# The experts' stage as a row of weight-unit steps in a fixed order, with float32 weights left unsplit in two down blocks of the light experts

## The chip, the cores and the metric

One NeuronCore of a Trainium2 chip runs the kernel. The engines are TensorE (PE in the profile, with PEld for its weight loads), VectorE (DVE), ScalarE (ACT), GpSimd (POOL) and the DMA queue that SyncE (SP) feeds. The metric is the time of one execution on the device in microseconds (us), as the median of repeated runs.

## The reference

Two encoder layers over 256 tokens of width 1024. Each has a token mixer, a cross-attention and a feed-forward part; in the second layer the feed-forward part is eight experts, of which each token uses two:

```python
def swiglu(t, w_gu, w_down):
    a, g = jnp.split(t @ w_gu, 2, axis=-1)
    return (jax.nn.silu(a) * g) @ w_down

def moe_swiglu(h, w_router, w_gu, w_down):
    ...
    top_logit, top_idx = lax.top_k(logits, TOP_K)
    ...
    for e in range(N_EXPERTS):
        out = out + gate[:, e:e + 1] * swiglu(t, w_gu[e], w_down[e])
```

Everything is float32. An expert's weights are 1024 x 5632 (gate and up) and 2816 x 1024 (down): 34.6 MB that have to be read whatever the number of tokens.

## The kernel before

**Split weights.** A product in float32 accuracy is built from `float32r` products (the profile writes fp32r). Each weight piece arrives by DMA in a buffer `raw`; ACT copies it rounded into `hi` (L216), DVE subtracts to get `lo = raw - hi` (L220), and TensorE multiplies with both. Pools give six buffers each for `hi` and `lo`, of 128 x 1024 elements, which is three units' worth; in the arm that ran there are nine buffers `raw` during the first expert and seven afterwards.

**Units.** A unit is one 1 MB piece (four blocks of 128 rows by 512 columns), so two pieces of `hi` and two of `lo`. An expert has six hidden blocks j; block 5 is half as wide. Per block there are two units of gate weights (tile `pm`, called g below), two of up weights (a) and two of down weights (d, tile `py`): 36 units an expert, six of them half as large, and 66 splits each on ACT and DVE.

**Heavy and light.** The experts are sorted by their number of tokens. The first three (heavy, up to 128 tokens) hold their activations as two parts and use three products per weight block (`mm3`, L234 to L236). The last five (light, up to 64 tokens) place high part and low part side by side in the 128 columns of one operand, so that two products do (`stream`, L915 and L916). The lower half of the result is then added to the upper one: ACT copies it out (`low`, L969) and a product with an identity adds it (L970). After that come `silu` on ACT (L950), the product `h` on DVE (L951), a transposition on PE (L954), and its split into `hTh` and `hTl` on ACT and DVE (L256 and L257).

**Pairs.** Two experts at a time, the tokens are collected by products with a selection matrix (`gather`, tiles `pg`, `xg`) and given back by another one (`scatter`, tile `psct`).

**Order.** The code writes an expert's work block by block. What stands behind a product (`low`, `silu`, ...) is put on the list `later` and run by `flush` after the splits of the next units have been written. The scheduler of the language decides the final order within each engine. DMA issues stand on SP's queue and wait only for a free buffer `raw`.

Of the kernel before, what the change touches and what calls it, by code (L numbers as in the profile page):

```python
# [21 lines left out]
DFF, E = 2816, 8  # L22
# [7 lines left out]
PLAIN = ()  # L30
# [126 lines left out]

class K:
# [29 lines left out]
    def unit(self, src, base, pk, c, g, blocks=False, whole=False):  # L188

# [8 lines left out]
        if isinstance(base, int):  # L198
            w = bass.AP(tensor=src.tensor, offset=src.offset + base + pk.off[c, g], ap=[[n, 128], [1, n]])
        else:  # L200

            o = base[1] + pk.off[c, g]
            w = src.rearrange("(e n) -> e n", e=E)[bass.ds(base[0], 1), o:o + 128 * n]
            w = w.rearrange("o (p n) -> (o p) n", p=128)
        nc.sync.dma_start(raw.rearrange("p k c -> p (k c)"), w)
        if whole:
            return [(k0, kn, raw)]
# [630 lines left out]
    def experts(self, c, pos, gs, xs, acc, A, ahead, full, early=()):  # L838


        down, self.later = None, []
        for e in range(E):
            if e % 2 == 0:
                pair = ahead
            name = self.nc.values_load(self.of[0:1, e:e + 1], engines=[mybir.EngineType.SP], min_val=0, max_val=E - 1)
            one = dict(pair, e=e, i=e % 2, xe=pair["xg"][e % 2], light=e >= full, name=name)
            for j in range(6):
                if e == 1 and j == 0:
# [6 lines left out]
                if e % 2 and e < E - 1 and j == 1:  # L855
                    ahead = self.gather(c, e + 1, pos, xs, A, full)
        self.down(*down, gs, acc, A)
        while self.later:
            self.flush()

    def gather(self, c, e, pos, xs, A, full):


        nc = self.nc
        half = CAP // 2
        light = [e + i >= full for i in range(2)]
        sl = A.tile([128, 2, 2, CAP], FR, name="sl")
        for t in range(2):
            for i in range(2):
                at = pos[:, t, e + i:e + i + 1]  # L870
                if light[i]:
                    nc.vector.tensor_scalar(sl[:, t, i].rearrange("p (a b) -> p a b", a=2),  # L872
                                            self.io[:, None, :half].to_broadcast([128, 2, half]), at, None,
                                            op0=OP.is_equal)
                else:
                    nc.vector.tensor_scalar(sl[:, t, i], self.io[:, CAP * c:CAP * c + CAP], at, None, op0=OP.is_equal)

        xg = []
        for i in range(1 if all(light) else 2):
            pool, tag = self.xgs[0]  # L880
            xg.append(pool.tile([128, 2, 8, CAP], FR, name="xg", tag=tag, bufs=1))
            self.xgs.append(self.xgs.pop(0))
        xg = [xg[0][:, i] for i in range(2)] if all(light) else [z[:, 0] if l else z for z, l in zip(xg, light)]
        p = [None, None]
        for k in range(8):
            for i in range(2):
                if k % 2 == 0:
                    p[i] = self.mm.tile([128, 2, 2 * CAP], FT, name="pg", tag="mm")
                for t in range(2):
                    nc.tensor.matmul(p[i][:, k % 2], xs[i][:, t, k * 128:k * 128 + 128],  # L890
                                     sl[:, t].rearrange("p a b -> p (a b)"), start=not t, stop=bool(t))
            if k % 2:
                ks = slice(k - 1, k + 1)
                for i in range(2):
                    for z, copy in ((0, lambda o, v: nc.scalar.activation(o, v, AF.Copy)),
                                    (1, nc.vector.tensor_copy)):
                        if light[i]:
                            cs = slice(z * half, (z + 1) * half)
                            copy(xg[i][:, ks, cs], p[z][:, :, i * CAP:i * CAP + CAP][:, :, cs])
                        else:  # L900
                            copy(xg[i][:, z, ks], p[z][:, :, i * CAP:i * CAP + CAP])
        st = A.tile([128, 2, S], FR, name="st")
        p = self.ps.tile([128, 2, S], FT, name="pst", tag="t")
        for i in range(2):
            for t in range(2):
                nc.tensor.transpose(p[:, i, t * 128:t * 128 + 128], f32(sl[:, t, i]), self.idn)
        nc.vector.tensor_copy(st, p)
        return dict(sl=sl, st=st, xg=[[z] if l else [z[:, 0], z[:, 1]] for z, l in zip(xg, light)])

    def stream(self, ps, x, k, w, first, last):  # L910

        if len(x) == 2:
            self.mm3(ps, [z[:, k] for z in x], w, first, last)
        else:
            self.nc.tensor.matmul(ps, x[0][:, k], w[0], start=first, stop=False)  # L915
            self.nc.tensor.matmul(ps, x[0][:, k], w[1], start=False, stop=last)  # L916

    def up(self, x, j, A):

        nc, I = self.nc, self.I  # L920
        light = x["light"]
        n = P_GU.chunks[2 * j][1]
        nb = n // 128

        def product(c):
            p = self.mm.tile([128, 512], FT, name="pm", tag="mm")
            u = self.chunk(I["we"], (x["name"], 0), P_GU, c)
            self.flush()
            for k0, kn, hi, lo in u:
                for k in range(kn):  # L930
                    self.stream(p[:, :n], x["xe"], k0 + k, (hi[:, k], lo[:, k]), k0 + k == 0, k0 + k == 7)
            return p

        pg = product(2 * j + 1)
        if light:
            self.later.append(lambda: self.fold(pg, n, A))
        pa = product(2 * j)
        half = CAP // 2
        plain = light and j in PLAIN
        if plain:  # L940
            hT = [A.tile([128, 4, half], FT, name="hTf", bufs=2)]
        else:
            hT = [A.tile([128, 4, CAP], FR, name="hT" + z) for z in ("h" if light else "hl")]

        def rest():
            if light:
                self.fold(pa, n, A)
            m = half if light else CAP
            h = A.tile([128, 512], FT, name="h", bufs=1)
            nc.scalar.activation(h[:m, :n], pa[:m, :n], AF.Silu)  # L950
            nc.vector.tensor_tensor(h[:m, :n], h[:m, :n], pg[:m, :n], op=OP.mult)  # L951
            p = self.ps.tile([128, 4, 128], FT, name="pht", tag="t")
            for b in range(nb):
                nc.tensor.transpose(p[:, b, :m], h[:m, b * 128:b * 128 + 128], self.idn[:m, :m])  # L954
            if plain:
                nc.scalar.activation(hT[0][:, :nb], p[:, :nb, :m], AF.Copy)
            elif light:
                self.split(p[:, :nb, :m], hT[0][:, :nb, :half], hT[0][:, :nb, half:])
            else:
                self.split(p[:, :nb], *(z[:, :nb] for z in hT))  # L960

        self.later.append(rest)
        return hT

    def fold(self, ps, n, A):

        half = CAP // 2
        low = A.tile([128, 512], FR, name="low", bufs=1)
        self.nc.scalar.activation(low[half:, :n], ps[half:, :n], AF.Copy)  # L969
        self.nc.tensor.matmul(ps[:half, :n], self.one64[half:], low[half:, :n], start=False, stop=True,  # L970
                              skip_group_check=True)

    def flush(self):

        later, self.later = self.later, []
        for f in later:
            f()

    def down(self, x, j, hT, gs, acc, A):

        nc, I = self.nc, self.I
        e, i = x["e"], x["i"]
        base = (x["name"], P_GU.size)
        plain = x["light"] and j in PLAIN
        if j == 0:
            self.py = [self.ps.tile([128, 512], FT, name="py", tag="s") for _ in range(2)]
        for cc in range(2):
            u = self.unit(I["we"], base, P_DN, cc, j, whole=plain)
            self.flush()
            for k0, kn, *w in u:  # L990
# [19 lines left out]
    def scatter(self, st, e, acc, A):  # L1010
# [23 lines left out]
        if i:  # L1034
            self.later.append(add)
# [91 lines left out]
```

## Time and profile before

| | us |
|---|---|
| median of 3 runs (1634.14 to 1635.0) | 1634.14 |
| the profiled execution's own time | 1637.31 |
| span of its trace | 1635.5 |
| PE busy / DVE busy / ACT busy | 1555.5 / 1304.2 / 1030.4 |

The experts' stage runs from about 847 us to the end of the span. A busy PE is not a PE at its peak: the profile draws a product of 512 columns some 0.4 us long, while in a dense row the next one starts 0.23 us later. A group of instructions on DVE is drawn the same way, so that its rate is read from long groups.

### The profile page before, as it was taken

To read this page: it belongs to the slowest core of one execution; us is meant where nothing else is said; L and a number is where in the kernel's file an instruction comes from. 1 tells how busy PE (TensorE), PEld (TensorE's weight loads), DVE (VectorE), ACT (ScalarE), POOL (GpSimd) and SP (SyncE) were. 2 spreads that over 40 slices of the span, in tenths; PEclk is the share of its full clock that TensorE was granted. 3 is DMA by queue.
4 is the path that set the end of the run, shared out by engine and by line. 5 is a ranking of instruction groups with operands and counts; after the bars stand their busy time and mean duration, and the time that the engine had idled before them with its cause. 6 is when DMAs were issued, how large, how long until landed. Compare 5 with 4: busy or idle time off the path is not lost.

```text
span 1635.5 us, 24155 instructions
## 1 busy us (share of the span) xinstructions
PE 1555.5 (95%) x8867; PEld 1276.5 (78%) x8867; DVE 1304.2 (80%) x1936; ACT 1030.4 (63%) x1422; POOL 32.9 (2%) x28
## 2 busy tenths in 40 slices
PE   6999999999999999999969999999999999999996
PEld 5999999899998889999858878888656556555554
DVE  7877686775545886777678888898899998999897
ACT  5665444544433575545436777777878788888884
POOL 1100000000000110000000000000000000000000
PEclk9999999999999999999979999999999999999999
DMA  7424564465555533456229798898999999999994
GB/s 275 142 104 144 186 247 158 155 223 190 181 180 184 190 121 126 149 199 230 79 100 426 310 405 328 334 363 321 395 335 394 381 356 371 342 405 345 406 374 147
DMA packets 65647, 421.32 MB, mean 258 GB/s; under 512 B 7664, under 2 KB 8560, under 8 KB 19568
## 3 DMA queue, kind: packets, MB, share of 16 engines
q1 hardware_dynamic: 65520, 419.69, 68.2%
q8 instruction: 72, 1.18, 0.3%
q14 instruction: 55, 0.45, 0.1%
HBM read 418.61 MB, written 1.05 MB: 257 GB/s over the span
## 4 chain that ended last, share of the span: by engine, by line
PE 78%; DVE 10%; ACT 5%; issue 5%; DMA 2%; POOL 0%; ACTq 0%; SPq 0%; DVEq 0%
PE pm L235 15%; PE pm L234 15%; PE pm L236 15%; PE pm L916 6%; DVE lo L220 6%; PE pm L915 4%; ACT hi L216 3%; PE psc L354 2%; PE py L234 2%; PE py L236 2%; PE py L235 2%; PE ptr L383 1%; PE pd L236 1%; PE pd L234 1%; PE pd L235 1%
## 5 line engine op out<-in xcount | busy, mean ns | idle before, releaser
L220 DVE TENSOR_TENSOR lo<-raw,hi 128x1024 fp32r<-128x1024 f32 (+2 forms) x1020 | 926.7, 955 | 187.2 <-ACT hi L216 183.7
L216 ACT ACTIVATE hi<-raw 128x1024 fp32r<-128x1024 f32 x770 | 770.1, 1052 | 255.9 <-PE pm L235 92.1
L236 PE MATMUL pm<-xTh,lo 128*128 128x256 f32 x928 | 264.5, 285 | 0.0
L234 PE MATMUL pm<-xTh,hi 128*128 128x256 f32 x928 | 264.4, 285 | 0.0
L235 PE MATMUL pm<-xTl,hi 128*128 128x256 f32 x928 | 264.3, 285 | 0.0
L916 PE MATMUL pm<-lo,xg 128*128 128x512 f32 (+1 forms) x480 | 197.1, 416 | 15.2 <-DVE lo L220 13.2
L915 PE MATMUL pm<-hi,xg 128*128 128x512 f32 (+1 forms) x480 | 181.8, 386 | 0.7 <-ACT hi L216 0.7
L235 PEld LDWEIGHTS pm<-xTl,hi 128*128 128x128 f32 x928 | 177.8, 192 | 1.1
L234 PEld LDWEIGHTS pm<-xTh,hi 128*128 128x128 f32 x928 | 177.7, 191 | 1.0
L236 PEld LDWEIGHTS pm<-xTh,lo 128*128 128x128 f32 x928 | 177.9, 192 | 0.7
L916 PEld LDWEIGHTS pm<-lo,xg 128*128 128x128 f32 x480 | 91.0, 190 | 88.8 <-DVE lo L220 77.6
L235 PE MATMUL pm<-lo,xg 128*128 128x512 f32 (+1 forms) x288 | 108.7, 377 | 2.3 <-DVE lo L220 2.0
L234 PE MATMUL pm<-hi,xg 128*128 128x512 f32 (+1 forms) x288 | 108.5, 377 | 1.8 <-DVE sl L872 1.8
L236 PE MATMUL pm<-hi,xg 128*128 128x512 f32 (+1 forms) x288 | 108.1, 375 | 0.0
L916 PE MATMUL py<-lo,hTh 128*128 128x512 f32 x220 | 94.7, 433 | 12.2 <-DVE lo L220 11.6
L915 PEld LDWEIGHTS pm<-hi,xg 128*128 128x128 f32 x480 | 91.2, 191 | 18.5 <-issue 5.6
L915 PE MATMUL py<-hi,hTh 128*128 128x512 f32 x220 | 91.1, 414 | 0.2 <-ACT hi L216 0.2
L950 ACT ACTIVATE h<-pm 64x512 f32<-64x512 f32 (+3 forms) x48 | 26.9, 560 | 85.2 <-PE pm L236 69.3
L916 PEld LDWEIGHTS py<-lo,hTh 128*128 128x128 f32 x220 | 40.9, 188 | 41.2 <-DVE lo L220 34.1
L969 ACT ACTIVATE low<-pm 64x512 fp32r<-64x512 f32 (+1 forms) x60 | 33.5, 558 | 61.4 <-PE pm L916 58.6
L235 PEld LDWEIGHTS pm<-lo,xg 128*128 128x128 f32 x288 | 54.9, 191 | 13.6 <-DVE lo L220 4.0
L234 PEld LDWEIGHTS pm<-hi,xg 128*128 128x128 f32 x288 | 54.8, 190 | 12.4 <-issue 2.0
(321 smaller groups left out, 2645.1 us busy)
## 6 DMA issues: line engine op xcount, KB each, us to landing
raw<-in_we SPq DMA_DIRECT2D x240, 1024.0 KB, 7.4
raw<-in_wm SPq DMA_DIRECT2D x84, 1024.0 KB, 4.8
raw<-in_wf SPq DMA_DIRECT2D x32, 1024.0 KB, 4.8
raw<-in_we SPq DMA_DIRECT2D x48, 512.0 KB, 4.5
gb<-in_lnv SPq DMA_DIRECT2D x14, 512.0 KB, 4.9
raw<-in_wm SPq DMA_DIRECT2D x4, 832.0 KB, 5.5
memr<-in_memT SPq DMA_DIRECT2D x3, 1024.0 KB, 4.7
bias<-in_bias SPq DMA_DIRECT2D x8, 256.0 KB, 4.3
```

Of the source, the lines that this page charges most:

```text
L216: nc.scalar.activation(hi, raw[:, ks, cs], AF.Copy)
L220: nc.vector.tensor_tensor(lo[:, kk], raw[:, a:][:, kk, cs], f32(hi[:, kk]), op=OP.subtract)
L234: t.matmul(out, a[0], b[0], start=first, stop=False, **kw)
L235: t.matmul(out, a[0], b[1], start=False, stop=False, **kw)
L236: t.matmul(out, a[1], b[0], start=False, stop=last, **kw)
L354: self.nc.tensor.matmul(p[:, t], q[i][a][:, t * 128:(t + 1) * 128], k[i][b], start=i + a + b == 0, stop=i == n - 1 and a == 1)
L383: nc.tensor.transpose(pt[:, kt, t * 128:(t + 1) * 128], e[:, t, kt * 128:(kt + 1) * 128], self.idn)
L915: self.nc.tensor.matmul(ps, x[0][:, k], w[0], start=first, stop=False)
L916: self.nc.tensor.matmul(ps, x[0][:, k], w[1], start=False, stop=last)
L950: nc.scalar.activation(h[:m, :n], pa[:m, :n], AF.Silu)
L969: self.nc.scalar.activation(low[half:, :n], ps[half:, :n], AF.Copy)
```

## The change

The experts' stage is written anew as one list of units over all eight experts. For each unit n the code writes a step: the products of unit n, the `hi` split of unit n+3, the `lo` split of unit n+2, the work that earlier steps have put down for step n, and the load of unit n+4. `Chain` ties each instruction of TensorE, VectorE and ScalarE to the one written before it on the same engine, so that these three engines issue in the order of the code; SP's loads are not tied. `later(n + d, f)` puts the instructions that `up`, `fold`, `down`, `gather` and `scatter` held into the steps n + d. In the light experts the down blocks 1 and 4 (`PLAIN`) are not split: the transposed hidden values are kept as one float32 tile `hTf` of 64 columns, and each block of weights gives one product of `hTf` and `raw`, both plain float32, instead of two float32r ones. In the last expert, six down units stand at the end. Its results are scattered as soon as each half is complete.

```diff
-PLAIN = ()
+PLAIN = (1, 4)
...
+class Chain:
...
+        def call(*args, **kw):
+            with self.tc.issue_after(self.last) if self.last else ExitStack():
+                r = f(*args, **kw)
+            self.last = r.ins
+            return r
...
-                hT = self.up(one, j, A)
-                self.cuts = 1
-                if down:
-                    self.down(*down, gs, acc, A)
-                down = (one, j, hT)
...
+        for e in range(E):
             for j in range(6):
+                units += [(e, z, j, g) for z in "ga" for g in range(2)]
+                at = (e, j - 1) if j else (e - 1, 5)
+                if at[0] >= 0 and (e, j) < (E - 1, 4):
+                    units += [(at[0], "d", at[1], g) for g in range(2)]
+        units += [(E - 1, "d", j, g) for j, g in ((3, 0), (3, 1), (4, 0), (5, 0), (4, 1), (5, 1))]
...
+        def split(n, z):
+            v = u[n]
+            if v["plain"]:
+                return
+            v[z] = [self.wp.tile([128, b - a, v["cn"]], FR, name=z, tag=z, bufs=6) for a, b in v["parts"]]
...
+                if v["plain"]:
+                    nc.tensor.matmul(p[:CAP // 2], a[0][:, at], v["raw"][:, k], start=False, stop=False)
+                    continue
...
+                products(n)
+                if n + 3 < len(units):
+                    split(n + 3, "hi")
+                if n + 2 < len(units):
+                    split(n + 2, "lo")
+                x = slots[e]
+                if kind == "g" and g:
+                    self.fold(n, 1, x["g"], u[n]["cn"], A, x)
+                if kind == "a" and g:
+                    self.hidden(n, x, j, u[n]["cn"], A, (e, j) == (E - 1, 5))
+                if kind == "d":
+                    self.down(n, x, j, g, gs, acc, A)
...
+            while n in todo:
+                f, args = todo[n].pop(0)
...
+                f(*args)
+            if n + 4 < len(units):
+                load(n + 4)
+            n += 1
...
+        self.fold(n, not fast, pa, cn, A, x)
+        for d, f in zip((1, 1, 2, 2, 3) if fast and light else (0, 0, 1, 1, 2) if fast else
+                        (1, 1, 3, 3, 4) if light else (0, 1, 2, 2, 3), (silu, times, turn, high, low)):
+            self.later(n + d, f)
```

In the changed kernel every chained instruction carries line 169, that of `call`. The following rows show the order of instructions at three places of the seventh expert (a light one).

On ACT, around one hidden block, the order before (`hi` the splits, `low` the half to be added, first for g and then for a, `h` the `silu`, `hTh` the transposed hidden values):

```order
L216 ACTIVATE hi<-raw 128x1024 x6
L969 ACTIVATE low<-pm 64x512
L216 ACTIVATE hi<-raw 128x1024 x4
L969 ACTIVATE low<-pm 64x512
L950 ACTIVATE h<-pm 64x512
L216 ACTIVATE hi<-raw 128x1024 x2
L256 ACTIVATE hTh<-pht 128x4x64
```

and in the changed kernel, from the copy of block 1 (`hTf`) to that of block 2:

```order
L169 ACTIVATE hTf<-pht 128x256
L169 ACTIVATE low<-pm 64x512
L169 ACTIVATE hi<-raw 128x1024 x2
L169 ACTIVATE low<-pm 64x512
L169 ACTIVATE hi<-raw 128x1024 x2
L169 ACTIVATE h<-pm 64x512
L169 ACTIVATE hi<-raw 128x1024 x4
L169 ACTIVATE hTh<-pht 128x4x64
```

The `silu` no longer stands directly behind the second `low`: a unit's `hi` is between them, and two units' between it and the copy of the transposition. Between the two `low` there are two `hi` instead of four, since the down units of block 1, which follow block 2's products, have none.

On DVE, after the gate values of the same expert, the order before:

```order
L220 TENSOR_TENSOR lo<-raw,hi 128x1024 x9
L951 TENSOR_TENSOR h<-h,pm 64x512
L220 TENSOR_TENSOR lo<-raw,hi 128x1024 x2
L257 TENSOR_TENSOR hTh<-pht,hTh 128x4x64
L220 TENSOR_TENSOR lo<-raw,hi 128x1024 x10
L951 TENSOR_TENSOR h<-h,pm 64x512
```

and in the changed kernel (the first `h` is that of block 2, in the step of block 1's first down unit):

```order
L169 TENSOR_TENSOR lo<-raw,hi 128x1024 x6
L169 TENSOR_TENSOR h<-h,pm 64x512
L169 TENSOR_TENSOR lo<-raw,hi 128x1024 x6
L169 TENSOR_TENSOR hTh<-pht,hTh 128x4x64
L169 TENSOR_TENSOR lo<-raw,hi 128x1024 x6
L169 TENSOR_TENSOR h<-h,pm 64x512
```

The `hTh` between the two is the subtraction that gives the low half of block 2's transposed values; it stands three units behind `h` now, and one behind it before. Ahead of the first `h` eight `lo` follow the `h` of block 1 (these six and two that stand further up), where there were twelve, and block 1 has no such subtraction.

On PE, the down units of a block before, with the addition of `low` (L970) and the transposition (L954) among their products:

```order
L915 MATMUL py<-hi,hTh 128x512
L916 MATMUL py<-lo,hTh 128x512
L970 MATMUL pm<-low,one_9158 64x512
L915 MATMUL py<-hi,hTh 128x512
L916 MATMUL py<-lo,hTh 128x512
...
L954 MATMUL pht<-idn,h 128x64 x4
L915 MATMUL py<-hi,hTh 128x512
```

and at the unsplit down units of the changed kernel:

```order
L169 MATMUL pm<-hi,xg 128x512
L169 MATMUL pm<-lo,xg 128x512
L169 MATMUL py<-raw,hTf 64x512 x4
L169 MATMUL pm<-low,one_9158 64x512
L169 MATMUL py<-raw,hTf 64x512 x4
L169 MATMUL pm<-hi,xg 128x512
L169 MATMUL pm<-lo,xg 128x512
```

The addition of `low`, for which `silu` waits, now stands behind the first of the two unsplit units.

## Rows read from the trace of the kernel before

**Rows 1.** The page: span; busy time, share and instructions of engines.

```profile
span 1635.5 us, 24155 instructions
PE 1555.5 (95%) x8867; PEld 1276.5 (78%) x8867; DVE 1304.2 (80%) x1936; ACT 1030.4 (63%) x1422; POOL 32.9 (2%) x28
```

**Rows 2.** Gate products, tile pgt: durations (ns, min/median/max), first and last start.

```profile
L1002 PE MATMUL pgt<-gs,sl x16: 164/208/250, 888.3 to 1553.0; 128*128 128x2 f32 x16
```

**Rows 3.** Windows between these gate products: experts 3 to 6, rest of 7.

```profile
core 0: us, PE busy (x) PEld busy (x) DVE busy (x) ACT busy (x) POOL busy (x), PEclk, DMA share, GB/s
...
1178.30:1274.10 95.80, 88.92 (x357) 55.90 (x356) 87.92 (x98) 76.86 (x97) 0.00 (x0) 1.00 0.93 362
1274.10:1366.10 92.00, 85.81 (x331) 53.17 (x330) 83.63 (x85) 76.93 (x97) 0.00 (x0) 0.98 0.96 374
1366.10:1461.70 95.60, 88.86 (x357) 55.88 (x356) 87.18 (x94) 76.80 (x97) 0.00 (x0) 1.00 0.94 365
1461.70:1553.00 91.30, 84.84 (x317) 51.33 (x316) 83.11 (x83) 76.03 (x93) 0.00 (x0) 0.98 0.96 374
1553.00:1618.40 65.40, 60.99 (x237) 37.40 (x235) 59.12 (x60) 52.87 (x66) 0.00 (x0) 1.00 0.84 314
```

**Rows 4.** PE timeline in a heavy expert: same place of two neighbouring blocks.

```profile
916.37 0.39 PE L234 MATMUL py<-hi,hTh 128*128 128x512 f32 x1
...
933.30 0.39 PE L234 MATMUL py<-hi,hTh 128*128 128x512 f32 x1
```

**Rows 5.** Groups by line, 1461.7 to 1553.0: busy, mean ns, idle before, releasers.

```profile
L220 DVE TENSOR_TENSOR lo<-raw,hi 128x1024 fp32r<-128x1024 f32 x67 | 77.9, 1219 | 5.4 <-ACT hi L216 5.4
L216 ACT ACTIVATE hi<-raw 128x1024 fp32r<-128x1024 f32 x67 | 65.6, 1049 | 0.1
L969 ACT ACTIVATE low<-pm 64x512 fp32r<-64x512 f32 x10 | 5.9, 593 | 10.1 <-PE pm L916 10.1
L951 DVE TENSOR_TENSOR h<-h,pm 64x512 f32<-64x512 f32 x5 | 3.4, 680 | 3.1 <-ACT h L950 3.1
```

**Rows 6.** DVE timeline, one block of a light expert: start, us, [idle before, releaser].

```profile
1476.41 0.68 DVE L951 TENSOR_TENSOR h<-h,pm 64x512 f32<-64x512 f32 x1 [0.61 <-ACT h L950]
1477.36 2.36 DVE L220 TENSOR_TENSOR lo<-raw,hi 128x1024 fp32r<-128x1024 f32 x2 [0.27 <-ACT hi L216]
1479.64 0.41 DVE L257 TENSOR_TENSOR hTh<-pht,hTh 128x256 fp32r<-128x256 f32 x1
1479.97 6.89 DVE L220 TENSOR_TENSOR lo<-raw,hi 128x1024 fp32r<-128x1024 f32 x6
1487.37 4.63 DVE L220 TENSOR_TENSOR lo<-raw,hi 128x1024 fp32r<-128x1024 f32 x4 [0.51 <-ACT hi L216]
1492.60 0.68 DVE L951 TENSOR_TENSOR h<-h,pm 64x512 f32<-64x512 f32 x1 [0.60 <-ACT h L950]
```

**Rows 7.** ACT timeline in the same block.

```profile
1478.44 5.79 ACT L216 ACTIVATE hi<-raw 128x1024 fp32r<-128x1024 f32 x6
1485.66 0.59 ACT L969 ACTIVATE low<-pm 64x512 fp32r<-64x512 f32 x1 [1.43 <-PE pm L916]
...
1491.97 0.59 ACT L950 ACTIVATE h<-pm 64x512 f32<-64x512 f32 x1 [0.54 <-PE pm L970]
```

**Rows 8.** PE timeline in the light expert: two products and the next one.

```profile
1472.79 0.39 PE L915 MATMUL pm<-hi,xg 128*128 128x512 f32 x1
1473.02 0.40 PE L916 MATMUL pm<-lo,xg 128*128 128x512 f32 x1
1473.25 0.40 PE L915 MATMUL pm<-hi,xg 128*128 128x512 f32 x1
```

**Rows 9.** PE timeline before the experts: eight float32 transpositions of 128 columns.

```profile
827.89 1.03 PE L311 MATMUL pt<-idn,x 128*128 128x128 f32 x8
```

**Rows 10.** DMA, 1500 to 1553: GB/s in 40 slices, whole, issues.

```profile
GB/s 250 213 213 244 204 145 402 445 420 260 192 402 359 445 383 414 427 424 396 436 380 424 427 427 433 408 439 439 402 445 420 420 439 414 414 414 402 396 420 371
DMA packets 3073, 19.89 MB, mean 375 GB/s; under 512 B 337, under 2 KB 337, under 8 KB 958
...
raw<-in_we SPq DMA_DIRECT2D x18, 1024.0 KB, 7.8
```

**Rows 11.** PE timeline: the last product of the last expert.

```profile
1617.94 0.39 PE L916 MATMUL py<-lo,hTh 128*128 128x512 f32 x1
```

More of the change, by code (lines that the diff above doesn't have):

```diff
@@ L836, in sort, with experts @@
         return out
-    def experts(self, c, pos, gs, xs, acc, A, ahead, full, early=()):
-        down, self.later = None, []
+    def experts(self, c, pos, gs, xs, acc, A, pair, full, early):
+        nc = self.nc
+        units = []
         for e in range(E):
[L843 to L846, printed above, removed]
@@ new lines, in experts, with load @@
+        self.later = later
+        u = [None] * len(units)
+        def load(n):
+            e, kind, j, g = units[n]
+            if e not in slots:
+                slots[e] = dict(e=e, i=e % 2, light=e >= full, hT={}, name=nc.values_load(
+                    self.of[0:1, e:e + 1], engines=[mybir.EngineType.SP], min_val=0, max_val=E - 1))
+                if e == 1:
+                    self.raws = [z for z in self.raws if z not in early]
+            pk, c, g, o = (P_DN, g, j, P_GU.size) if kind == "d" else (P_GU, 2 * j + (kind == "g"), g, 0)
+            cn, (k0, kn) = pk.chunks[c][1], pk.groups[g]
+            pool, tag = self.raws[0]
+            self.raws.append(self.raws.pop(0))
+            raw = pool.tile([128, kn, cn], FT, name="raw", tag=tag, bufs=3 if pool is self.wp else 1)
+            o += pk.off[c, g]
+            w = self.I["we"].rearrange("(e n) -> e n", e=E)[bass.ds(slots[e]["name"], 1), o:o + 128 * kn * cn]
+            nc.sync.dma_start(raw.rearrange("p k c -> p (k c)"), w.rearrange("o (p n) -> (o p) n", p=128))
+            kp = 1024 // cn
+            u[n] = dict(raw=raw, k0=k0, kn=kn, cn=cn, plain=kind == "d" and slots[e]["light"] and j in PLAIN,
+                        parts=[(k, min(kn, k + kp)) for k in range(0, kn, kp)])
@@ new lines, in experts @@
+        for n in range(4):
+            load(n)
+        for n in range(3):
+            split(n, "hi")
+        for n in range(2):
+            split(n, "lo")
+        n = 0
+        while n < len(units) or todo:
+            if n < len(units):
+                e, kind, j, g = units[n]
+                if (kind, j, g) == ("g", 0, 0):
+                    if e % 2 == 0 and e:
+                        pair = ahead
+                    slots[e].update(pair, xe=pair["xg"][e % 2])
+                if (kind, j, g) == ("g", 1, 0) and e % 2 and e < E - 1:
+                    ahead, acts = self.gather(c, e + 1, pos, xs, A, full, self.ps, "o")
+                    for d, f in acts:
+                        later(n + d, f)
+                products(n)
[8 more added lines that the diff above has]
+                    self.hidden(n, x, j, u[n]["cn"], A, (e, j) == (E - 1, 5))
+                if kind == "d":
+                    self.down(n, x, j, g, gs, acc, A)
+            else:
+                nc = self.nc
+            while n in todo:
+                f, args = todo[n].pop(0)
+                if not todo[n]:
+                    del todo[n]
+                f(*args)
+            if n + 4 < len(units):
+                load(n + 4)
+            n += 1
@@ L865, in gather @@
+    def gather(self, c, e, pos, xs, A, full, pool, tag):
         half = CAP // 2
         light = [e + i >= full for i in range(2)]
-        sl = A.tile([128, 2, 2, CAP], FR, name="sl")
-        for t in range(2):
-            for i in range(2):
[L870 to L876, printed above, removed]
@@ L902, in gather @@
[L902 to L916, printed above, removed]
@@ L918, in up @@
[L918 to L963, printed above, removed]
@@ new lines, in gather, with fold, low, add @@
+        return r, acts + [(25, back), (26, back2)]
+    def fold(self, n, late, ps, cn, A, x):
+        if not x["light"]:
+            return
+        half = CAP // 2
+        hold = []
+        def low():
+            hold.append(A.tile([128, 512], FR, name="low", bufs=1))
+            self.nc.scalar.activation(hold[0][half:, :cn], ps[half:, :cn], AF.Copy)
+        def add():
+            self.nc.tensor.matmul(ps[:half, :cn], self.one64[half:], hold[0][half:, :cn], start=False, stop=True,
+                                  skip_group_check=True)
+        self.later(n, low)
+        self.later(n + late, add)
```

284 lines of the change are left out of this document (180 added, 104 removed).

## The prediction

> **What bounds the kernel now.** The page comes first: DVE is busy 80% of the span, PE 95% [rows 1]. These are averages over stages, and the change touches only the experts. So I cut that stage into periods at the gate products, of which each expert has one pair, from 888.3 to 1553.0 us [rows 2].
>
> A heavy expert is bound by TensorE. From one block to the same place of the next, 933.30 - 916.37 = 16.93 us pass [rows 4]. The 72 products that lie between them, at 0.23 us each, take 16.5. The change leaves these products as they are.
>
> A light expert takes 91.3 and 92.0 us, or 95.8 and 95.6 where tokens of the next pair are also collected and given back [rows 3]. DVE is busy 83.1 of 91.3 us there and 87.2 of 95.6, so the pair's work costs it 4.1. PE looks nearly as busy, but its products are drawn longer than their interval: the next starts after 0.23 us [rows 8]. By intervals a light expert's PE work is about 71 us: 248 products of 512 columns take 57, 32 of half the width 4, the additions, transpositions and half a pair's products some 10.
>
> The groups by line say what DVE's idle 8.2 us wait for: `lo` waits 5.4 us for `hi`, and `h` 3.1 us for ACT [rows 5]. DVE's timeline shows these gaps in each block, 0.61, 0.27 and 0.51 us, and 16.2 us from `h` to `h` [rows 6]. ACT's timeline has the reason: it has made six `hi` ahead, then stands at `low` for 1.43 us until TensorE has finished the product, and `hi` is queued behind [rows 7]. Three engines wait for each other in turns, and the one with most work, DVE, loses 9%.
>
> The DMA is the fourth party. Its busy share is 0.94 to 0.96 at a mean of 362 to 374 GB/s [rows 3]. But ACT waits for nothing else than PE in those groups, and the slices from 1515 us on stay near 414 GB/s, single ones up to 445 [rows 10]. An expert's 34.6 MB at 414 GB/s are 83.6 us. That is the floor for whatever I take from DVE.
>
> **The change part by part.**
>
> *Splits removed.* Per light expert, two blocks have two down units of two pieces each: eight `hi` and eight `lo` fall away, and two subtractions of transposed values. The interval of `lo` in a long group is (6.89 - 1.22)/5 = 1.13 us, with 1.22 the mean of one [rows 5, 6]; the subtraction's is 0.33 [rows 6]. That is 9.0 + 0.7 = 9.7 us off DVE, leaving 83.1 - 9.7 = 73.4. ACT loses eight intervals of 0.95 ((5.79 - 1.05)/5, [rows 5, 7]), from 76.0 to 68.4; it is not the bound.
>
> *Products exchanged.* Thirty-two fp32r products per expert become 16 plain float32 ones. No row has such a product. The nearest float32 row is a transposition of 128 columns, eight in 1.03 us, that is 0.107 each [rows 9], which would be 0.43 us for 512 columns; nothing excludes that it runs as an fp32r product, 0.23. For the other end: this kernel takes three fp32r products for a product of two split operands, and a full one has four, 4 x 0.23 = 0.93. A transposition only moves values, while a product has to multiply all their bits, so I take 0.93. PE then has 16 x 0.93 - 32 x 0.23 = 7.5 us more, some 78 per expert. The Trainium skill says the same for true float32 ("FP8 and Floating Point Precision", section "TensorE Precision Notes": four passes, high and low half of each operand). By the transpositions' rate the sum below would be 13 us lower, by four passes it stays; no run here shows it yet.
>
> *Where these products stand.* They come in pairs of units, 3.7 us each, during which TensorE frees no `hi` or `lo`. Take the end of the unit ahead as zero. DVE is then 0.95 ahead (four products at 0.23). It makes the next `lo` unit (2.27) until 1.3. Next in its order is `h`; that waits for `silu`, which waits for the addition behind the first unsplit unit: 3.7 + 0.24 + 0.7 for `silu` gives 4.7, and with `h` 5.4. Two more `lo` units end at 9.9. The one after needs buffers of the first split unit behind the pair, which PE ends at 3.7 + 0.24 + 3.7 + 1.96 = 9.6; its `hi` takes 1.1 and its `lo` 2.3, so 13.0. Without the pair DVE would be there at -0.95 + 4 x 2.27 + 0.68 = 8.8. The loss is 4.2 us a pair, 8.4 an expert. In general it is 8 times the product's price, less 3.2; at 0.43 it is about 1, since `h` alone is late then.
>
> *The fixed order.* In each step `hi` of unit n+3 and `low` both wait for the end of unit n, so ACT has no wait that was not its own already. The `lo` of that unit is due two units (4.5 us) later; `hi` takes 1.9 of these. So the 8.2 us idle should mostly go. I leave 2.0 in, as ACT has 68 us of work and any `low`, `silu` or `ysh` may push a `hi`.
>
> A light expert thus takes 73.4 + 8.4 + 2.0 = 83.8 us, or 87.9 with a pair's work. This is just above the DMA's 83.6, and above PE's 78. The buffers `raw` of the unsplit units are held until their products end; with seven of them, 2.5 us each at 414 GB/s, three or four still lie in the queue. Four periods go from 374.7 to 343.4: -31.3.
>
> *The last expert.* From its gate products to the last product, 1553.0 to 1618.3, it takes 65.3 us [rows 2, 11]. Up to the end of block 5's products DVE now has 34 `lo` (38.5), four `h` and two subtractions (3.2), and one pair's loss (4.2), less a start 1.3 ahead: 44.6. Then come six down units, now on TensorE: two of 2.3 at DVE's rate and a lag of 0.9, two of 3.7 unsplit, two halves of 1.0, in all 14.9. That is 59.5, or -5.8. Half of the scatter falls before the end: -1.5.
>
> *The rest.* At the start, the selection matrices of the second pair no longer stand ahead of the first `lo`: -0.7. Heavy experts 0: their steps are 2.8 us of PE against 2.3 of DVE, which covers the order; without that cover each 0.1 us a step would cost 3.6 us an expert.
>
> The sum is -39.3 against the profiled execution's 1637.3: 1598.0. That execution lies 3.2 above the median of 1634.14, so I predict 1595.
>
> **The rivals.**
>
> *Float32 products are cheap* (0.43 or less). Loss per pair 1, so DVE has 73.4 + 2 + 2 = 77.4, below the DMA's floor. Periods are then 83.6, four times: -40 instead of -31.3, the last expert -11: 1582. For it speak the transpositions' rate; against it, that they do not multiply.
>
> *The order stalls*, because three units of buffers are too few where products, splits and `silu` interlock as they do at the pairs. If 8 us an expert stay idle as before and a pair costs 6, a light expert takes 73.4 + 8.2 + 12 = 93.6, as long as before; half way, some 18 us are gained: 1616. The waits of ACT for PE [rows 7] speak for it.
>
> *The DMA is the bound already.* A share of 0.96 speaks for it. Then the 374 GB/s stay, periods without pair's work remain at 92 us, those with it fall by 3, and the last expert gains its 7: 1621. Against it: the 414 GB/s over nearly 40 us, and that no group waits for a load. The Trainium skill's "DMA: Bandwidth & Descriptors", section "Specifications", gives about 358 GB/s as a core's limit from HBM, by which a light expert could not fall below 97 us and the change would give nothing; this trace does not agree, with 374 as a mean and 414 over long stretches.
>
> *Slower.* The float32 product is dearer. A mean light expert takes 93.7; without any pair's loss it would be 77.5. A loss of 8.1 a pair eats that, at a price of 8 x - 3.2 = 8.1, so 1.4 us a product. At 1.86, twice what I take, the loss is 11.7, the periods grow by 7 us each and the last expert, whose end has two such units on TensorE, by 8: 1670. No row speaks for it, none excludes it.
>
> **How the numbers follow.** Chances: forecast 0.60 (1587 to 1605), cheap products 0.11, stalls 0.16, DMA bound 0.05, dear products 0.08. 0.2% (3 us) is about what a measurement of this kernel can tell from no change. Of the stalls and the DMA case about 0.04 lie within it, the rest is faster: faster 0.87, same 0.04, slower 0.09 (with a little of the stalls). For 8 in 10 the range takes in the cheap products and the stalls up to their half-way price: 1575 to 1616.
>
> **What would show it.** Right: `py<-raw,hTf` at an interval near 0.93 us; 58 `lo` per light expert instead of 66; gate products some 84 and 88 us apart; heavy blocks still 16.9 us; DVE's longest waits at `h` behind an unsplit unit and at the third unit after the pair; DMA at 390 to 413 GB/s. Wrong: another interval of that product; ACT waiting for `raw`; DVE idle at every block; heavy blocks longer than 17 us.

## The result and the profile after

| | before | after |
|---|---|---|
| median (4 runs each), us | 1634.57 (1634.14 to 1635.75) | 1605.6 (1604.05 to 1610.11) |
| ratio | | 0.9826 [0.9805, 0.9848] |
| span of the trace, us | 1635.5 | 1602.6 |

The change saves 29 us where 39 were forecast. In the spans it is 32.9, since the profiled execution of before lies above its median and that of the changed kernel below.

The page of the changed kernel answers to [rows 1]:

```profile
span 1602.6 us, 24173 instructions
PE 1539.1 (96%) x8867; PEld 1278.3 (80%) x8867; DVE 1258.1 (79%) x1886; ACT 1011.2 (63%) x1382; POOL 32.9 (2%) x28
```

VectorE has lost 46 us of work and TensorE leads by more than before. To see where the time went, I cut both traces at the last scaled output of an expert (`ysh` on ACT), which ends an expert's work in both orders. The stage up to the third heavy expert's output, and from there to the last light expert's, in the kernel before (columns as in [rows 3]):

```profile
848.00:1163.40 315.40, 310.49 (x1455) 254.39 (x1453) 274.25 (x293) 229.36 (x270) 0.00 (x0) 0.98 0.91 360
1163.40:1618.40 455.00, 423.24 (x1650) 263.15 (x1650) 414.24 (x431) 372.15 (x464) 0.00 (x0) 0.99 0.93 362
```

and in the changed one:

```profile
848.00:1157.90 309.90, 307.03 (x1459) 254.38 (x1459) 281.54 (x291) 244.17 (x272) 0.00 (x0) 0.99 0.94 369
1157.90:1585.50 427.60, 409.88 (x1644) 263.97 (x1645) 361.48 (x385) 337.68 (x421) 0.00 (x0) 0.99 0.95 383
```

So 5.5 us come from start and heavy experts and 27.4 from the light ones; what follows the last output takes 17.1 us in both. Of the 27.4, the last expert gives 5.1 (79.6 to 74.5) and the four others 22.3: they took 94.9, 92.9, 94.7 and 92.9 us and take 88.6, 87.9, 88.1 and 88.5. Between gate products, as in [rows 3], the four periods are

```profile
1172.10:1262.00 89.90, 86.57 (x362) 57.44 (x361) 76.89 (x85) 72.71 (x93) 0.00 (x0) 1.00 0.94 382
1262.00:1346.90 84.90, 81.22 (x324) 51.93 (x324) 71.95 (x77) 68.75 (x84) 0.00 (x0) 1.00 0.97 392
1346.90:1438.50 91.60, 88.19 (x362) 58.35 (x361) 78.32 (x85) 72.33 (x93) 0.00 (x0) 0.98 0.99 396
1438.50:1521.40 82.90, 80.75 (x318) 50.53 (x317) 69.94 (x71) 68.31 (x83) 0.00 (x0) 1.00 0.97 389
```

where 87.9 and 83.8 had been forecast. These marks alternate more than the others, because a pair's scattering now falls between an expert's last output and the next gate product; I take the outputs. DVE is idle for 13 us of each period. TensorE is drawn nearly full: over the last three of the four experts it is idle 3.7 us an expert.

PE's timeline of the changed kernel at a pair of unsplit units (no such row existed before):

```profile
1449.13 0.39 PE L169 MATMUL pm<-lo,xg 128*128 128x512 f32 x1
1449.45 3.65 PE L169 MATMUL py<-raw,hTf 128*64 128x512 f32 x8
1453.03 0.45 PE L169 MATMUL pm<-low,one 64*64 64x512 f32 x1
1453.40 3.65 PE L169 MATMUL py<-raw,hTf 128*64 128x512 f32 x8
1456.98 0.50 PE L169 MATMUL pm<-hi,xg 128*128 128x512 f32 x1
```

From a unit's first product to what follows it are 3.58 us for four products, 0.895 each. (A plain float32 product leaves two records, hence x8.) DVE's timeline there, beside [rows 6], and ACT's, beside [rows 7]:

```profile
1446.36 3.49 DVE L169 TENSOR_TENSOR lo<-raw,hi 128x1024 fp32r<-128x1024 f32 x3
1454.13 0.68 DVE L169 TENSOR_TENSOR h<-h,pm 64x512 f32<-64x512 f32 x1 [4.28 <-ACT h L169]
1454.74 6.88 DVE L169 TENSOR_TENSOR lo<-raw,hi 128x1024 fp32r<-128x1024 f32 x6
```

```profile
1450.23 2.00 ACT L169 ACTIVATE hi<-raw 128x1024 fp32r<-128x1024 f32 x2
1453.51 0.59 ACT L169 ACTIVATE h<-pm 64x512 f32<-64x512 f32 x1 [1.27 <-PE pm L169]
1454.01 1.99 ACT L169 ACTIVATE hi<-raw 128x1024 fp32r<-128x1024 f32 x2
1457.98 2.01 ACT L169 ACTIVATE hi<-raw 128x1024 fp32r<-128x1024 f32 x2 [1.99 <-PE pm L169]
```

The late `h` is there: DVE stands 4.28 us until the addition behind the first unsplit unit and `silu` are through (4.67 and 4.23 us in the two experts before). The small gaps before `lo` of [rows 6] are nearly gone, six `lo` in one row, but at most other blocks `h` still waits 1.3 to 2.1 us for ACT. The other pair, of block 4, looks different. Its additions are of half the width, and `h` waits 1.4 us there. What waits long there is a `lo` (2.4 to 3.7 us in the three experts), for a `hi` that waits for its load; here ACT and then DVE:

```profile
1313.75 2.00 ACT L169 ACTIVATE hi<-raw 128x1024 fp32r<-128x1024 f32 x2 [3.24 <-DMA raw<-in_we]
1314.84 2.36 DVE L169 TENSOR_TENSOR lo<-raw,hi 128x1024 fp32r<-128x1024 f32 x2 [3.68 <-ACT hi L169]
```

Over the three experts ACT waits for loads and TensorE for `low`:

```profile
ACT hi L169 <- DMA raw<-in_we: 9.6, 5, 3.2
PE pm L169 <- ACT low L169: 1.6, 3, 0.9
```

In e1 below, with every block split, ACT waits 0.9 us for loads.

### The profile page after: what moved, and what is told of

It reads as the page before. It is cut to its first block, busy times and chain, and to the rows that moved or that the text cites. A ratio compares the mean times of both kernels' runs of the same rounds, so it can differ in the third digit from the quotient of the medians.

```text
span 1602.6 us, 24173 instructions
## 1 busy us (share of the span) xinstructions
PE 1539.1 (96%) x8867; PEld 1278.3 (80%) x8867; DVE 1258.1 (79%) x1886; ACT 1011.2 (63%) x1382; POOL 32.9 (2%) x28
## 4 chain that ended last, share of the span: by engine, by line
PE 86%; DVE 7%; ACT 3%; issue 2%; DMA 2%; POOL 0%; SPq 0%; ACTq 0%; DVEq 0%
PE pm L169 23%; PE py L169 13%; PE pm L252 11%; PE pm L253 11%; PE pm L254 11%; DVE lo L169 3%; PE psc L372 2%; ACT hi L169 1%; PE ptr L401 1%; PE pd L254 1%; PE pd L252 1%; PE pd L253 1%; PE pp L252 1%; DVE lo L238 1%; PE pht L169 1%
## 5 line engine op out<-in xcount | busy, mean ns | idle before, releaser
L169 DVE TENSOR_TENSOR lo<-raw,hi 128x1024 fp32r<-128x1024 f32 x488 | 572.3, 1215 | 29.8 <-ACT hi L169 21.1
L169 ACT ACTIVATE hi<-raw 128x1024 fp32r<-128x1024 f32 x488 | 495.1, 1054 | 92.4 <-PE pm L169 52.4
L238 DVE TENSOR_TENSOR lo<-raw,hi 128x512 fp32r<-128x512 f32 (+1 forms) x484 | 314.2, 683 | 155.9 <-ACT hi L234 153.0
L234 ACT ACTIVATE hi<-raw 128x1024 fp32r<-128x1024 f32 (+1 forms) x242 | 253.4, 1054 | 250.6 <-PE pm L253 92.2
L169 PE MATMUL pm<-hi,xg 128*128 128x512 f32 (+1 forms) x1056 | 358.6, 384 | 2.1 <-ACT hi L169 2.1
L169 PEld LDWEIGHTS pm<-hi,xg 128*128 128x128 f32 x1056 | 197.3, 190 | 50.9 <-issue 16.1
L169 PE MATMUL py<-raw,hTf 128*64 128x512 f32 x160 | 73.0, 599 | 0.0
L169 DVE TENSOR_TENSOR h<-h,pm 64x512 f32<-64x512 f32 (+3 forms) x48 | 30.4, 634 | 47.9 <-ACT h L169 47.9
L169 PEld LDWEIGHTS py<-hi,hTh 128*128 128x128 f32 x272 | 51.2, 188 | 14.7 <-issue 4.2
L169 PE MATMUL py<-hi,hTl 128*128 128x512 f32 x132 | 52.4, 397 | 0.0
```

Source lines behind the costliest of these rows:

```text
L169: r = f(*args, **kw)
L234: nc.scalar.activation(hi, raw[:, ks, cs], AF.Copy)
L238: nc.vector.tensor_tensor(lo[:, kk], raw[:, a:][:, kk, cs], f32(hi[:, kk]), op=OP.subtract)
```

## The experiments

Each was timed against the kernel before on its own chip. The ratio is what is compared; a step of 0.001 is 1.6 us.

| | us | ratio to before |
|---|---|---|
| e1 order alone | 1599.85 | 0.9774 [0.9757, 0.9791] |
| e2 unsplit blocks alone | 1642.62 | 1.0041 [1.0028, 1.0054] |
| e3 earlier addition | 1610.94 | 0.9849 [0.9837, 0.9862] |
| e4 fewer products | 1596.46 | 0.9765 [0.9749, 0.9782] |
| e5 no `lo` | 1568.85 | 0.9590 [0.9575, 0.9604] |
| e6 everything at once | 1665.21 | 1.0179 [1.0165, 1.0194] |
| e7 merged half units | 1605.89 | 0.9816 [0.9803, 0.9830] |
| e8 six raw buffers | 1609.05 | 0.9835 [0.9822, 0.9849] |
| e9 more products | 1612.55 | 0.9868 [0.9852, 0.9883] |
| e10 half the unsplit products | 1585.67 | 0.9695 [0.9680, 0.9710] |
| e11 held buffers | 1602.59 | 0.9809 [0.9796, 0.9823] |
| e12 one unsplit block | 1603.23 | 0.9805 [0.9792, 0.9818] |

**The two parts apart (e1, e2).** The changed kernel without unsplit blocks, and the kernel before with them:

```diff
-PLAIN = (1, 4)
+PLAIN = ()
```

> The changed kernel with every down block split again: the fixed order alone. Theory V (VectorE is the bound of a light expert, and what the pairs of unsplit units cost is its late h): no pair loss, no relief, so 83.1 + 2 = 85 us without and 89 with a pair's work, some 1.5 us an expert slower than the changed kernel: 1610. Theory T (TensorE, dense in the changed kernel's light experts, is the bound there): TensorE gets back 7.0 us an expert, VectorE becomes the bound again at the same 85 and 89: a shade slower without pair, faster with it, 1603. Theory M (the loads are the bound, 83 to 85 us an expert): as the changed kernel, 1605. If instead the order alone gives nothing, 1634.

```diff
-PLAIN = ()
+PLAIN = (1, 4)
```

> The kernel before, in its own order, with down blocks 1 and 4 of the light experts unsplit. V: VectorE loses 9.7 of 83 us an expert; the waits for ScalarE stay and the pairs cost some 4 us each, so little is left: 1625 to 1634. T: TensorE has 7 us more an expert, in an order in which it also waits for low: 1625 or slower than before. M: no gain beyond 84 us an expert, 1605 to 1615.

The order alone is better than the whole change, and the unsplit blocks cost time in either order: 0.0041 in the old one, 0.0052 in the new. The window over three light experts in e1:

```profile
1246.50:1506.40 259.90, 245.59 (x1018) 169.42 (x1017) 253.42 (x268) 234.81 (x286) 0.00 (x0) 0.97 0.99 401
```

and in the changed kernel:

```profile
1246.50:1511.00 264.50, 253.50 (x1018) 164.01 (x1017) 225.31 (x238) 211.65 (x262) 0.00 (x0) 0.99 0.98 393
```

In e1 DVE is busy 97.5% and a light expert takes 86.6 us; the unsplit blocks take 28 us off DVE over the three experts, and yet each expert takes 1.5 us longer. In e2 the waits of the three light experts say where TensorE's long units arrive:

```profile
ACT low L969 <- PE pm L916: 53.9, 36, 3.6
DVE h L951 <- ACT h L950: 28.5, 18, 4.1
```

**Is it the late `h`? (e3)** The addition is moved between the second and third product of the first unsplit unit:

```diff
                     nc.tensor.matmul(p[:CAP // 2], a[0][:, at], v["raw"][:, k], start=False, stop=False)
+                    if g == 0 and k == 1:
+                        for i, (f, args) in enumerate(todo.get(n, [])):
+                            if f.__name__ == "addlow":
+                                todo[n].pop(i)
+                                f(*args)
+                                break
...
```

> The changed kernel with the addition of low moved up, between the second and third product of the first unsplit unit, so that silu and h come 1.8 us earlier at each pair; the same work. V: h's wait falls from 4.3 to 2.5 us at each of ten pairs, and 15 us are gained: 1590. T: VectorE's wait at h costs nothing, less than 3 us gained: 1603 to 1606. M: 1605.

No gain. The edit did less than it was meant to: `silu` stands behind a unit's `hi` on ACT, so at this pair the wait of `h` fell only from 4.28 to 3.07 us, and over three experts DVE's waits at `h` did not fall at all (28.7 us before the edit, 30.5 with it). What was given back here was lost at the next `hi`, which waits for TensorE to come through the pair, 3.23 us instead of 1.99. So e3 does not show what an earlier `h` alone would be worth:

```profile
1454.03 0.59 ACT L169 ACTIVATE h<-pm 64x512 f32<-64x512 f32 x1
1454.53 1.99 ACT L169 ACTIVATE hi<-raw 128x1024 fp32r<-128x1024 f32 x2
1459.75 2.01 ACT L169 ACTIVATE hi<-raw 128x1024 fp32r<-128x1024 f32 x2 [3.23 <-PE pm L169]
```

**Is it TensorE's time? (e4, e9, e10)** e4 leaves out, in light experts, the `lo` product of the first weight block of each split unit, so that part of the low weights is missing from the result:

```diff
-                    nc.tensor.matmul(p, a[0][:, at], w[1], start=False, stop=kk == last)
+                    if k != 0:
+                        nc.tensor.matmul(p, a[0][:, at], w[1], start=False, stop=kk == last)
```

> The changed kernel without the lo product of the first weight block of each split unit in the light experts (left out of the result; all loads and splits stay): TensorE has 6.9 us less per light expert, nothing else changes. T: periods with a pair's work fall from 90 to about 84, those without to the loads' 82, in all 15 to 25 us: 1580 to 1590. V: VectorE's work and its waits stay; 0 to 4 us from earlier frees: 1601 to 1605. M: 1605.

e9 splits every block and issues the products of blocks 1 and 4 twice, so that they count twice in the result; e10 is the whole change with half of the unsplit products, which are missing from the result:

```diff
                     nc.tensor.matmul(p, a[0][:, at], w[1], start=False, stop=kk == last)
+                    if kind == "d" and j in (1, 4):
+                        for z in w:
+                            nc.tensor.matmul(p, a[0][:, at], z, start=False, stop=False)
```

> The new order with every block split, and in the light experts every product of the down blocks 1 and 4 issued twice (so that those blocks count twice in the output): a unit there takes TensorE 3.7 us, as an unsplit one does, while its raw buffer is freed as early as ever. The order with all blocks split took 1599.9, the whole change 1605.6. If the whole change loses those 6 us to TensorE's longer units: 1606 or, since VectorE keeps all its work here, up to 1616. If it loses them to the raw buffers that its unsplit units hold for longer: 1598 to 1602.

```diff
+                if v["plain"] and k % 2:
+                    continue
                 if v["plain"]:
```

> The whole change with two of the four products of each unsplit unit left out (so half of those blocks is missing from the output): the unit takes 1.8 us as a split one does, its raw buffer is held until TensorE comes to it all the same. If TensorE's longer units cost the time: 1590 to 1597, like the run with fewer products. If the held buffers do: 1602 to 1606.

e9 and e10 show that the time of the products at the pair costs. e9 loses 0.0094 against e1 with nothing changed but 7 us an expert of products, and no `h` in its three experts waits longer than 2.4 us, so the loss needs no late `h`. e10 regains 0.0131. e4 regains 0.0061, less than was expected if TensorE's sum alone were the bound. e4 and e10 take about as much from TensorE (6.9 and 7.2 us an expert) and leave DVE the same work, yet e10 gains twice as much: it counts most at the pair, where the other engines are standing. The windows over three light experts of e9 and e4, where TensorE is idle 3.5 and 7.0 us an expert:

```profile
1245.60:1513.80 268.20, 257.58 (x1114) 188.95 (x1113) 253.89 (x268) 235.26 (x286) 0.00 (x0) 0.98 0.96 388
1246.70:1507.30 260.60, 239.55 (x922) 147.95 (x920) 225.15 (x238) 211.45 (x261) 0.00 (x0) 0.98 0.99 399
```

In e4 the period is only 1.3 us shorter than in the changed kernel; the next limit lies close behind. The window of e10:

```profile
1244.40:1497.80 253.40, 236.34 (x970) 158.06 (x969) 224.84 (x238) 211.30 (x261) 0.00 (x0) 0.99 1.00 412
```

84.5 us an expert: with products at half the price, the relief of DVE pays after all.

**Is it the buffers? (e8, e11)** e8 is e1 with six buffers `raw` instead of seven; e11 is e1, but ACT reads a column of the raw piece again when TensorE uses that unit, so that it comes free as late as an unsplit one:

```diff
-                    self.arm(0, pos, gs, xs, x, A, ahead, FULL, T[2:], 4)
+                    self.arm(0, pos, gs, xs, x, A, ahead, FULL, T[2:], 3)
```

> The fixed order with every block split and six buffers raw instead of seven after the first expert. The unsplit units hold two buffers two to three steps longer. If that is what made the whole change slower than the order alone, one buffer fewer costs at least the same, 5 us or more: 1605 to 1615. If TensorE's 7 us more made it, little: 1600 to 1602.

```diff
+                if kind == "d" and x["light"] and j in (1, 4):
+                    held = A.tile([128, 1], FT, name="held", bufs=2)
+                    nc.scalar.activation(held, u[n]["raw"][:, u[n]["kn"] - 1, :1], AF.Copy)
```

> The new order with every block split; in the light experts ScalarE reads one column of raw of the down blocks 1 and 4 again at the step of that unit's products, so that these buffers come free as late as those of unsplit units, at about 0.2 us of ScalarE's time each, 0.8 an expert. If the held buffers cost the time: 1604 to 1609. If TensorE's longer units do: 1599 to 1602.

Buffers do cost something: one less for good costs 0.0061 against e1, holding four per expert longer 0.0035 (5.7 us), part of which is the ACT work itself. The median of e11 lies between its two expectations. In its trace three light experts take as long as in the changed kernel (264.5), but TensorE is held up in another way, by `low`:

```profile
1243.40:1507.70 264.30, 244.52 (x1012) 170.15 (x1010) 253.80 (x268) 235.64 (x297) 0.00 (x0) 0.97 0.98 396
PE pm L169 <- ACT low L169: 11.8, 11, 2.3
```

In the changed kernel this wait is 1.6 us. So held buffers are enough for such a loss where DVE keeps its work; in the changed kernel ACT does wait for loads, but TensorE hardly feels it, and e10 holds the buffers too and is the fastest of all that keep DVE's splits elsewhere. Some of the loss may still be the buffers'.

**One block (e12).**

```diff
-PLAIN = (1, 4)
+PLAIN = (4,)
```

> The whole change with one unsplit block (4) instead of two. If the loss goes with the number of blocks: half way, 1602 to 1603.5. If one block's relief of VectorE (4.9 us an expert) is worth more than its 3.5 us of TensorE, because VectorE is the bound with none and TensorE only with two: 1590 to 1597, which would be the best version.

Between none and two, with no optimum in between. Its interval lies just above that of e1; the step from one block to two, 0.0021, is within the intervals. That fits a loss that goes with the number of blocks.

**How fast can the loads go? (e5)** The order alone, without `lo` splits and products in light experts (that share of the result is missing):

```diff
-            if v["plain"]:
+            if v["plain"] or z == "lo" and slots[units[n][0]]["light"]:
                 return
...
-                w = [v[z][m][:, k - v["parts"][m][0]] for z in ("hi", "lo")]
+                w = [v[z][m][:, k - v["parts"][m][0]] for z in (("hi", "lo") if len(a) == 2 else ("hi",))]
...
```

> The fixed order with every block split, but in the light experts no lo at all: neither the splits on VectorE nor their products (left out of the result; all loads and hi stay). VectorE has some 75 us and TensorE 28 us less per light expert, ScalarE some 65 us of work left. Theory M (the loads are the floor that the fixed order reached, 86 us an expert at 400 GB/s with slower stretches at the half-size units): the periods stay at 84 to 86 us: 1590 to 1598. Theory V/T (an engine's work is the bound at 86): the periods fall to the 77 us that 34.6 MB take at 445 GB/s or to ScalarE's 70: 1545 to 1565.

The DMA in its light stage, 40 slices of 6 us:

```profile
GB/s 429 425 427 418 429 430 430 415 427 430 421 429 419 430 430 430 423 426 425 430 422 422 427 426 427 427 423 430 425 427 425 431 423 429 420 431 425 420 431 426
DMA packets 15514, 103.56 MB, mean 426 GB/s; under 512 B 1726, under 2 KB 1726, under 8 KB 4030
```

The loads ran at 426 GB/s, no slice below 415, and an expert took 81.0 us. Neither e1 (401 GB/s) nor the changed kernel (393) is there, so the 86 us that one theory took was not the loads' floor. Whether 81.0 us is that floor is not shown. ACT is busy 233.5 of 243.1 us here and waits little for loads, while the loads' queue (SPq) waits for buffers that ACT has to free:

```profile
ACT hi L169 <- DMA raw<-in_we: 3.5, 12, 0.5
SPq L891 <- ACT hi L169: 142.0, 84, 2.8
```

So ScalarE may be what bounds this run.

**What in the order gives the gain (e6, e7).** e6 is e1 with addition, `silu` and `h` in the step in which they come up, not one later, and the transposition and its split two steps earlier:

```diff
-        self.later(n + late, add)
+        self.later(n, add)
...
-                        (1, 1, 3, 3, 4) if light else (0, 1, 2, 2, 3), (silu, times, turn, high, low)):
+                        (0, 0, 1, 1, 2) if light else (0, 1, 2, 2, 3), (silu, times, turn, high, low)):
```

> The fixed order with every block split, but in the light experts the addition, silu, h, transposition and its split follow as directly as before: ScalarE's order is then low, silu, hi x2, hTh, hi x6 again, word for word that of the kernel before. Theory W (the gain came from moving these, since hi stood behind a low and a silu that waited for TensorE): VectorE's gaps of 1.4 to 1.6 us a block return, 8 us an expert: 1628 to 1636. Rival: the gain came from the look-ahead of two and three units: 1600 to 1605.

It is 29 us slower than before, beyond both expectations. On ACT `low` stands behind four `hi`, and the addition behind `low` on TensorE, with the next products now tied behind it. ACT, then TensorE:

```profile
1289.04 3.90 ACT L169 ACTIVATE hi<-raw 128x1024 fp32r<-128x1024 f32 x4 [1.42 <-PE pm L169]
1292.96 0.59 ACT L169 ACTIVATE low<-pm 64x512 fp32r<-64x512 f32 x1
```

```profile
1293.61 0.45 PE L169 MATMUL pm<-low,one 64*64 64x512 f32 x1 [1.65 <-ACT low L169]
```

Over three light experts these waits of TensorE add up:

```profile
PE pm L169 <- ACT low L169: 47.0, 36, 2.5
```

They are 4.9 us in e1. So the gain is not in fixing an order: a fixed order without the delays loses. It is in giving each result of another engine a unit's time before TensorE asks for it.

e7 is e1 with block 5's two half-size gate (and up) units merged into one of 1 MB:

```diff
-                units += [(e, z, j, g) for z in "ga" for g in range(2)]
+                units += [(e, z, j, g) for z in "ga" for g in range(j == 5, 2)]
...
```

> The fixed order with every block split; the gate and up weights of block 5, which lay as two half-size units each, are laid out and loaded as one unit of 1 MB with rows of 8 KB a partition (same weights, same work, 34 units an expert). M with slower half-size transfers: four of six half-size units an expert go, some 1 to 2 us an expert: 1590 to 1596. If the slow stretches are not due to the size: 1599 to 1601.

Slower by 0.0042, so nothing is gained by larger loads. That the small units were no bottleneck does not follow, for with two steps fewer the delays (counted in units) no longer fit: a new wait appears.

```profile
PE py L173 <- DVE hTh L173: 10.3, 3, 3.5
```

## Why the prediction came out as it did

The forecast of 1595 was 10.6 us too low, with the measured time inside its range and just above the 1587 to 1605 that had most of the chances. Between the profiled executions the sum missed by 6.4 (-32.9 for -39.3); the rest is that these two lie 2.7 above (before) and 1.1 below (after, 1604.5) their medians.

*Right.* The float32 product: 0.93 taken, 0.895 measured, close to four of the 0.23 us of [rows 8]. The Trainium skill ("FP8 and Floating Point Precision", "TensorE Precision Notes") says four passes, and this trace agrees. e10 stands for the rival of cheap products: 1582 was worked out, 1585.7 measured. The heavy blocks: 16.97 us from transposition to transposition (918.96 to 935.93), 16.93 in [rows 4]. The last expert: -5.1 between outputs, for -5.8; by the gate products, as it was forecast, it is -1.4 (65.4 to 64.0 up to the last output), because these now come earlier against the outputs.

*Order.* Forecast 8.2 - 2.0 = 6.2 us per light expert. Over the last three of the four experts the mean was 93.5 before and is 86.6 in e1: 6.9.

*Unsplit blocks: the step that failed.* "Splits removed" and the "pairs" together were -9.7 + 8.4 = -1.3 us per expert; e1 and the changed kernel show +1.5. The 2.8 between them make 11 us over four experts; the order, start and heavy experts gave some of it back. That is luck for the number: the forecast had 0.7 of the 5.5 us that start and heavy experts gave. The work taken from DVE is there (28 us in three experts, 9.4 each). The loss that was set against it is larger: DVE is idle 13.1 us an expert and 2.2 in e1, so the pairs cost it 10.9 for 8.4. The forecast had 3.4 us at `h` and 0.8 at a later `lo` of each pair; at the first pair `h` waited 4.2 to 4.7, at the second only 1.4, behind a `lo` that waited 2.4 to 3.7 for a late load. What was missed first is in "PE is at 78": that sum left TensorE too much room. It put additions, transpositions and half a pair's products at some 10 us an expert, without rows for them. PE's timeline of the changed kernel shows an addition among products:

```profile
1446.72 0.39 PE L169 MATMUL pm<-lo,xg 128*128 128x512 f32 x1
1447.04 0.45 PE L169 MATMUL pm<-low,one 64*64 64x512 f32 x1
1447.41 0.50 PE L169 MATMUL pm<-hi,xg 128*128 128x512 f32 x1
1447.75 0.40 PE L169 MATMUL pm<-lo,xg 128*128 128x512 f32 x1
```

From 1446.72 to 1447.75 are 1.03 us, less two products of 0.23: 0.57 for the addition, because the product after it starts late and hands on late too. Four transpositions cost 0.79 in the same way (1442.26 to 1443.51, less 0.46):

```profile
1442.26 0.39 PE L169 MATMUL pm<-lo,xg 128*128 128x512 f32 x1
1442.79 0.46 PE L169 MATMUL pht<-idn,h 64*128 64x64 f32 x4
1443.18 0.50 PE L169 MATMUL pm<-hi,xg 128*128 128x512 f32 x1
1443.51 0.39 PE L169 MATMUL pm<-lo,xg 128*128 128x512 f32 x1
```

With twelve additions (two of half width, 0.45) and six transpositions (one 0.46), these are 11.0 us an expert. Then 216 products of 0.23, 32 of 0.12 and 16 of 0.895 make 67.8: 79 without the pair's work, whose products (32 gatherings at 0.115 and 16 scatterings at 0.23) add 7.4 every other expert, 82.5 on average. The forecast had 78 on average, well below its DVE sum of 85.9; at 82.5, and with waits of its own, TensorE comes first, and the period is 88.2. Some of these waits came with the order:

```profile
PE psct L169 <- DVE hTh L169: 4.6, 2, 2.3
PE pg L169 <- DVE sl L169: 3.0, 1, 3.0
```

They stand in e1 in the same size, so they cost only where TensorE is the bound. That the products' time at the pairs is what the unsplit blocks lose is shown by e9 and e10; that TensorE's sum is not all of it, by e4. Of the 5.7 us between its 82.5 and the 88.2, 3.7 are drawn as waits of TensorE, 2.8 of them at the scattering, the gathering and the gate products and 0.7 for `low` and `lo`. The other 2.0 are not settled.

*Buffers.* The prediction let three or four loads lie in the queue while the unsplit units hold their buffers, and named ACT waiting for `raw` as a sign of being wrong. That sign is there, 9.6 us in three experts (0.9 in e1, none in e9), so this step failed too. The cost is hidden where TensorE is the bound: its waits for `low` and `lo` are 2.2 us in three experts.

*Small terms.* The start and the heavy experts gave 5.5 us where 0.7 was forecast: TensorE waited there for the selection matrix (1.8) and for `lo` (2.0), but these add up to only part of it; the cause of the rest is open. The tail gave 0 for -1.5: what follows the last expert's output takes as long as before, whether half of the scatter is done or not.

*Rivals.* "The order stalls" said that 8 us an expert stay idle and a pair costs 6. The first is refuted by e1 (2.2 us idle); the second was nearer than the forecast, 5.5 us of DVE's time a pair (half of 10.9) for 4.2. "DMA is the bound already" is refuted by e5, "dear products" by 0.895 us. The Trainium skill's "DMA: Bandwidth & Descriptors", section "Specifications", puts a core's limit from HBM near 358 GB/s; 426 over 243 us in e5 do not agree.

## What to carry to other kernels

Add up every engine by starts, not by the width of its products: an addition of 512 columns among other products took 0.57 us here, where the next product of a dense row starts after 0.23. With such terms and its waits TensorE had no room left. Before moving work from the fullest engine to the next one, do half of the change alone: e1, the order without the unsplit blocks, is the best version found and beats both kernels by its interval. And when an order is fixed by hand, what counts is the distance between a result and its use on the next engine: with the distances one or two units shorter (e6) the same order lost 65 us.

## What the hardware showed unexpectedly

The DMA's busy share hardly tells how fast the loads go: 393, 401, 412 and 426 GB/s were all seen at shares of 0.98 to 1.01. In e5 the granted clock of TensorE was 0.81 as a mean of the light stage, where TensorE's drawn busy time was 71% and it waited for `low` 58.3 us of 243; in the changed kernel it was 0.99. ScalarE or the loads bound that stretch, so the time does not show what the clock costs.

```profile
1237.40:1480.50 243.10, 172.74 (x595) 115.95 (x594) 32.07 (x69) 233.50 (x285) 0.00 (x0) 0.81 1.01 426
```
